# Gated-branch projection by seven products: where the partial sums of a pair of column blocks are kept

## The chip, the core and the metric

The kernel runs on one core of one Trainium2 chip. The metric is the device time of one execution in microseconds (us); several runs are taken and the median stands for the kernel. Five engines take part: TensorE (PE, matmuls into PSUM, with its weight loads PEld), VectorE (DVE), ScalarE (ACT), GpSimd (POOL) and SyncE (SP, which only issues DMAs). Each engine works through its own queue in order, and semaphores tie the queues together. SBUF holds the tiles; PSUM is eight banks of 128 x 512 fp32, which PE writes and DVE and ACT read and write.

## What is computed

One block of an encoder, in fp32, for 1024 positions of width 1024 (`norm` is an RMS norm, `mod` six vectors from a small conditioning input):

```python
h = rms_norm(x, norm_mix_g) * (1.0 + sc1) + sh1
b_s, c_s, v_s, v_c, gl_c, gate_br = split(h @ w_in)            # 7 x 1024 columns
y_a = (b_s * causal_dwconv(c_s * v_s, conv_short_w)) @ w_short_out   # 3 taps
u   = causal_dwconv(v_c * sigmoid(gl_c), conv_conf_w) + conv_conf_b  # 31 taps
y_b = silu(layer_norm(u)) @ w_conf_out
g_a, g_b = split(sigmoid(gate_br))
x = x + g1 * ((g_a * y_a + g_b * y_b) @ w_o)
h2 = rms_norm(x, norm_ffn_g) * (1.0 + sc2) + sh2
a, b = split(h2 @ w_ffn_in)
x = x + g2 * ((silu(a) * b) @ w_ffn_out);  return rms_norm(x, final_norm_g)
```

## The kernel before

**Layout.** Activations lie transposed: channels on the 128 partitions, positions along the row, in two halves of 512 (`halves`). A weight unit is a tile of 128 x 1024. To keep fp32 accuracy each operand is split in a rounded high part and the rest (`wh` by ACT, line 219; `wl` by a subtraction, line 220), and every product is three matmuls: high x high (L314), high x low part of the activation (L315), low part of the weight x high (L317).

**The projection.** The first columns of `w_in` are done as plain products (tiles `lead` and `gb`). The other 48 blocks of 128 columns are done in twelve **duals**, counted from 0. A dual takes two pairs of column blocks, p = 0 and 1 (list `PAIRS`), and does each 2 x 2 block product with seven products instead of eight, in the order `PRODUCTS = "1265734"` (M1, M2, M6, M5, M7, M3, M4). A product has two halves, one for each pair, of 4 x 3 matmuls of 128 x 512. M1, M6, M7 and M4 add up in a bank called x, M5 and M3 in z, M2 stands alone in y: three banks for each of the two pairs, six in all, taken at M1, M2 and M5 from a pool of six, so that x, y and z keep their places from dual to dual. The other two PSUM banks (`c0`, `c1`) hold the sums of the long convolution.

**The four results of a pair** are M1+M2, M1+M6+M5+M3 and two more with M7 and M4. `win_evac` (lines 647 to 712) reads the banks after each half of a product. ACT copies x to SBUF after M1 and after M6 (L673) and z after M5 (L688); DVE adds y, x and z to those copies after M2, M7 and M3 (`plus`, L633). Then comes what the kind of pair wants: `p` (c_s and v_s) multiplies the two blocks (L637) and runs the three-tap convolution; `q` (two blocks of b_s) multiplies onto that convolution's result (L683, L637) and stores it; `u` (v_c and gl_c) makes a sigmoid on ACT and multiplies (L679, L703); `g` (gates) makes sigmoids (L685, L695, L701) and stores them. In lines 637, 679 and 703 the factor `z` or `sig` is a copy in SBUF, not the bank. `short_conv` (L622 to 628) scales a row of 1024 on ACT into an SBUF tile (L624) and adds two taps to it on DVE, 1024 wide (L626).

**Weights of a dual.** `dual_units` loads four blocks by SP and lets POOL make the sums of blocks (L239, L241, L243 and, for M3, L260) and all seven `wl`. A weight unit is asked for two products ahead (`AHEAD`); there are three `wh` and three `wl` buffers and five `raw` ones, so a unit's cast waits until the product three before it is done, and the loads of a dual wait until POOL has read the last unit of the one before. POOL's order is L239, L241, `wl` of M1, L243, `wl` of M2, L260, then `wl` of M6, M5, M7, M3, M4.

**The long convolution** (31 taps, eight channel blocks) runs on DVE meanwhile: two differences (L742, L743), one start (L756) and 46 taps (L751) a block, each tap a multiply-add of 128 x 512 with its sum in `c0` or `c1`. Their places in DVE's queue are given by `reads`, the list of the `plus` instructions: tap n of block j is put behind read `(j * 47 + n) * 70 / (8 * 47)` of 72. When a block is done, `add_conv` (L765 to 772) puts its store in ACT's queue (L769) and its two adds into `tot` in POOL's (L772), behind weight unit `(j + 1) * 70 * 7 / 48 + 5`, counted through the duals, seven to each.

**Late work.** Sigmoids that nobody waits for, and the stores of gates, are collected in `late` and issued with the next ACT copy of M1, M6 or M5 (`gates`, L641 to 645). A scheduler then merges the instructions of each engine into its queue under these orders.

Of the kernel before, what the change touches and what calls it, by code (L numbers as in the profile page):

```python
# [35 lines left out]
ALU = mybir.AluOpType  # L38

P = 128  # L40
# [53 lines left out]

CONV_READS = 70

# [24 lines left out]
def block_kernel(ctx: ExitStack, tc: tile.TileContext, x0, xT, c, vecs, ada, w_first, w_plain, w_duals,  # L121
# [499 lines left out]

    def short_conv(j, p):  # L622
        sc[j] = uc_tile(f"sc{j}", T)
        nc.scalar.activation(sc[j], p[:, :T], AF.Copy, scale=col(V_SW, j))  # L624
        for s in range(1, SK):
            nc.vector.scalar_tensor_tensor(  # L626
                out=sc[j], in0=p[:, s : s + T], scalar=col(V_SW + s * KC, j), in1=sc[j], op0=ALU.mult, op1=ALU.add
            )

    reads = []  # L630

    def plus(out, ps, b):
        reads.append(nc.vector.tensor_tensor(out, ps, b, ALU.add).ins)  # L633

    def minus_times(out, a, b):

        nc.vector.scalar_tensor_tensor(out=out, in0=a, scalar=-1.0, in1=b, op0=ALU.mult, op1=ALU.mult)  # L637

    late = []

    def gates(ins):  # L641

        with tc.issue_after(ins):
            while late:
                late.pop(0)()

    def win_evac(pairs):

        st = [{} for _ in pairs]

        def start(e, kind, j):
            if kind == "u":
                u.append(u_tile(j))
                e["b"] = [u[j][:, CK - 1 + h * H : CK - 1 + (h + 1) * H] for h in range(2)]
            elif kind == "p":
                e["p"] = uc_tile(f"p{j}", T + SK - 1)
                nc.vector.memset(e["p"][:, : SK - 1], 0.0)
                e["b"] = [e["p"][:, SK - 1 + h * H : SK - 1 + (h + 1) * H] for h in range(2)]
            elif kind == "g":
                e["t"] = [uc_tile("sig", T) for _ in range(2)]  # L660
                e["b"], e["c"] = ([t[:, s] for s in halves] for t in e["t"])

        def evac(i, m, ps):
            kind, j, *rest = pairs[i]
            e = st[i]
            if m == "1":
                start(e, kind, j)
                if kind == "q":
                    e["b"] = [g_tile("m")]
            if m == "6" and kind == "q":  # L670
                e["b"].append(g_tile("v"))
            if m in "16":
                gates(nc.scalar.copy(e["b"][m == "6"], ps).ins)  # L673
            elif m in "23":
                h = m == "3"
                b = e["b"][h]
                plus(b, ps, b)
                if kind == "u" and h:
                    nc.vector.tensor_tensor(b, b, e["z"], ALU.mult)  # L679
                elif kind == "p" and h:  # L680
                    minus_times(b, e["z"], b)
                elif kind == "q":
                    nc.vector.tensor_tensor(sc[j][:, halves[h]], b, sc[j][:, halves[h]], ALU.mult)  # L683
                elif kind == "g":
                    late.append(lambda: nc.scalar.activation(b, b, AF.Sigmoid))  # L685
            elif m == "5":
                e["z"] = e["c"][1] if kind == "g" else g_tile("z")
                gates(nc.scalar.copy(e["z"], ps).ins)  # L688
            elif m == "7":
                z = e["z"]  # L690
                plus(z, ps, z)
                if kind == "u":
                    nc.scalar.activation(z, z, AF.Sigmoid, scale=-1.0)
                elif kind == "g":
                    late.append(lambda: nc.scalar.activation(z, z, AF.Sigmoid, scale=-1.0))  # L695
                elif kind == "q":
                    minus_times(sc[j + 1][:, halves[1]], e["z"], sc[j + 1][:, halves[1]])
            else:
                if kind in "ug":
                    sig = e["c"][0] if kind == "g" else g_tile("sig")  # L700
                    nc.scalar.activation(sig, ps, AF.Sigmoid, scale=-1.0)  # L701
                if kind == "u":
                    nc.vector.tensor_tensor(e["b"][0], e["b"][0], sig, ALU.mult)  # L703
                elif kind == "p":
                    minus_times(e["b"][0], ps, e["b"][0])
                    short_conv(j, e["p"])
                elif kind == "q":
                    minus_times(sc[j + 1][:, halves[0]], ps, sc[j + 1][:, halves[0]])
                    for i in range(2):
                        q_store(j + i)  # L710
                else:
                    late.append(lambda: [nc.scalar.dma_start(gate_dram[g], t) for g, t in zip((j, *rest), e["t"])])
        return evac
# [7 lines left out]
    def q_split(j, h):  # L721

        hi, q = qT[j][h]
        nc.scalar.copy(hi, f32(q))
        with tc.issue_after(reads[-1]):
            nc.vector.tensor_tensor(q, f32(q), f32(hi), ALU.subtract)
# [7 lines left out]
    TAPS = CK // 2 * 3 + 2  # L734

    def conv(j):
# [4 lines left out]
        with tc.issue_after(reads[j * CONV_READS // KC]):  # L741
            nc.vector.tensor_tensor(d, ev, od, ALU.subtract)  # L742
# [4 lines left out]
        def tap(out, src, s, wt, acc):  # L747
            nonlocal n
            n += 1
            with tc.issue_after(reads[(j * TAPS + n) * CONV_READS // (KC * TAPS)]):  # L750
                tap.ins = nc.vector.scalar_tensor_tensor(  # L751
                    out=out, in0=src[:, s : s + H], scalar=wt, in1=acc, op0=ALU.mult, op1=ALU.add
                ).ins

        with tc.issue_after(reads[j * CONV_READS // KC]):
            nc.vector.tensor_scalar(a0, od[:, :H], wsum[:, j : j + 1], col(V_CB, j), ALU.mult, ALU.add)  # L756
# [8 lines left out]
    def add_conv(j):  # L765

        hi, lo = pool_los[min((j + 1) * CONV_READS * 7 // (6 * KC) + 5, 7 * n_duals + 1)]
        with tc.issue_after(hi):
# [565 lines left out]
```

## Time and profile before

| what | value |
|---|---|
| median of 3 runs | 1500.69 us (1497.21 to 1502.33) |
| the profiled execution | 1500.65 us, its span 1498.9 us |
| granted TensorE clock, mean | 0.994 |
| stage of the twelve duals | 110.51 to 582.76 us of the span |
| in that stage busy: DVE, ACT, POOL | 437.12, 164.67, 355.12 us |

The span runs from the first to the last instruction; the execution's time has 1.75 us around it. A row of a group reads: line, engine, operation, output<-inputs, shapes, count | busy us, mean ns of one | idle time of the engine before them and what ended it. A row of a timeline reads: start, us, engine, line, operation, and in brackets the idle time before it and what ended that. A row of waits reads: who <- whom: us in total, times, longest.

### The profile page before, as it was taken

How to read it: one execution, taken by the hardware profiler on the slowest of the kernel's cores; microseconds unless marked ns; L12 is line 12 of the kernel's file. 1: busy time of each engine (PE TensorE's matmuls, PEld its weight loads, DVE VectorE, ACT ScalarE, POOL GpSimd, SP SyncE). 2: the span in 40 equal slices, each digit the busy share in tenths (PEclk: the TensorE clock that was granted, in tenths of full speed). 3: DMA queues.
4: the chain of work that ended last, by engine and by line, in shares of the span. 5: the costliest groups of instructions: out<-in, count | busy, mean ns of one | idle time of the engine just before them, and what ended most of it. 6: DMA issues, size and time to landing. Idle time of an engine off the chain costs nothing.

```text
span 1498.9 us, 17818 instructions
## 1 busy us (share of the span) xinstructions
PE 1476.3 (98%) x6523; PEld 1212.1 (81%) x6523; DVE 1190.0 (79%) x1573; ACT 591.0 (39%) x845; POOL 557.6 (37%) x467
## 2 busy tenths in 40 slices
PE   8999999999999999999999999999999999999997
PEld 5888878878878878888888887888888888888887
DVE  7997898999999997759775699877777665677755
ACT  4753333333333235226334474444444443222235
POOL 0046777778788684310121101100010016544105
PEclk9999999999999999999999999999999999999999
DMA  9412213223212159447663525555554449998403
GB/s 355 169 62 71 99 57 126 71 85 98 90 52 93 48 180 362 156 159 239 199 217 115 160 96 196 186 181 171 182 180 163 150 150 356 364 315 258 144 24 113
DMA packets 82698, 243.26 MB, mean 162 GB/s; under 512 B 9521, under 2 KB 11697, under 8 KB 82610
## 3 DMA queue, kind: packets, MB, share of 16 engines
q1 hardware_dynamic: 41776, 133.91, 26.9%
q0 software_dynamic: 36944, 95.44, 19.3%
q10 hardware_dynamic: 3890, 12.78, 2.1%
q8 instruction: 51, 0.84, 0.2%
q14 instruction: 37, 0.30, 0.1%
HBM read 179.70 MB, written 62.39 MB: 162 GB/s over the span
## 4 chain that ended last, share of the span: by engine, by line
PE 87%; DVE 5%; POOL 4%; issue 1%; DMA 1%; ACT 1%; POOLq 0%; ACTq 0%; DVEq 0%
PE x L317 11%; PE x L314 11%; PE x L315 11%; PE z L314 6%; PE z L315 6%; PE z L317 6%; PE y L317 4%; PE y L314 4%; PE y L315 4%; PE ya L314 2%; PE yb L317 2%; PE yb L314 2%; PE ya L315 2%; PE ya L317 2%; PE yb L315 2%; POOL wl L220 2%
## 5 line engine op out<-in xcount | busy, mean ns | idle before, releaser
L219 ACT CAST wh<-raw 128x1024 fp32r<-128x1024 f32 (+2 forms) x248 | 250.2, 1009 | 482.8 <-PE z L315 111.7
L220 POOL TENSOR_TENSOR wl<-raw,wh 128x1024 fp32r<-128x1024 f32 x92 | 237.3, 2587 | 95.4 <-ACT wh L219 91.3
L220 DVE TENSOR_TENSOR wl<-raw,wh 128x1024 fp32r<-128x1024 f32 (+2 forms) x156 | 177.6, 1139 | 36.5 <-ACT wh L219 35.1
L751 DVE SCALAR_TENSOR_TENSOR c<-diff,vec,c 128x512 f32<-128x512 f32 x232 | 172.2, 750 | 4.0
L1050 POOL DMA_DIRECT2D hid<-stage x71 | 37.9, 534 | 347.4 <-DVE stage L354 340.8
L314 PE MATMUL x<-th,wh 128*128 128x512 f32 x336 | 130.9, 390 | 0.0
L317 PE MATMUL x<-th,wl 128*128 128x512 f32 x336 | 130.7, 389 | 0.0
L315 PE MATMUL x<-tl,wh 128*128 128x512 f32 x336 | 130.7, 389 | 0.0
L751 DVE SCALAR_TENSOR_TENSOR c<-u,wsum,c 128x512 f32<-128x512 f32 x112 | 84.0, 750 | 4.5 <-issue 2.5
L239 POOL TENSOR_TENSOR raw<-raw 128x1024 f32<-128x1024 f32 x12 | 29.5, 2455 | 128.6 <-DVE wl L220 91.4
L317 PE MATMUL x<-t2h,wl 128*128 128x512 f32 x184 | 72.4, 395 | 3.6 <-POOL wl L220 3.6
L314 PEld LDWEIGHTS x<-th,wh 128*128 128x128 f32 x336 | 63.1, 188 | 13.6 <-DVE z L633 0.3
L317 PEld LDWEIGHTS x<-th,wl 128*128 128x128 f32 x336 | 63.1, 188 | 13.1
L315 PEld LDWEIGHTS x<-tl,wh 128*128 128x128 f32 x336 | 63.1, 188 | 13.0
L314 PE MATMUL x<-t2h,wh 128*128 128x512 f32 x184 | 72.3, 394 | 1.2 <-ACT wh L219 1.2
L315 PE MATMUL x<-t2l,wh 128*128 128x512 f32 x184 | 72.1, 393 | 0.0
L353 ACT CAST stage<-g 128x512 fp32r<-128x512 f32 x62 | 38.3, 621 | 71.2 <-DMA hid<-stage 37.6
L314 PE MATMUL z<-th,wh 128*128 128x512 f32 x168 | 65.4, 389 | 0.0
L315 PE MATMUL z<-tl,wh 128*128 128x512 f32 x168 | 65.4, 389 | 0.0
L317 PE MATMUL z<-th,wl 128*128 128x512 f32 x168 | 65.4, 389 | 0.0
L354 DVE TENSOR_TENSOR stage<-g,stage 128x512 fp32r<-128x512 f32 x62 | 42.3, 687 | 27.1 <-ACT stage L353 27.0
L1076 POOL DMA_DIRECT2D th<-hid x71 | 38.1, 537 | 49.8 <-PE x L317 29.8
(840 smaller groups left out, 4089.6 us busy)
## 6 DMA issues: line engine op xcount, KB each, us to landing
hid<-stage POOLq DMA_DIRECT2D x71, 512.0 KB, 4.7
raw<-in_w_fi SPq DMA_DIRECT2D x51, 512.0 KB, 3.8
raw<-in_w_duals SPq DMA_DIRECT2D x48, 512.0 KB, 3.5
th<-hid POOLq DMA_DIRECT2D x71, 256.0 KB, 5.7
tl<-hid POOLq DMA_DIRECT2D x71, 256.0 KB, 5.8
ada<-in_ada SPq DMA_DIRECT2D x24, 512.0 KB, 6.2
raw<-in_ada SPq DMA_DIRECT2D x24, 512.0 KB, 4.4
raw<-in_w_fo SPq DMA_DIRECT2D x24, 384.0 KB, 5.7
```

Source lines behind the costliest of these rows:

```text
L219: hi = nc.scalar.copy(wh, raw)
L220: lo = lo_engine.tensor_tensor(wl, raw, f32(wh), ALU.subtract)
L239: eng.tensor_tensor(a["s1"], a["21"], a["22"], ALU.add)
L314: nc.tensor.matmul(ps, wh, xh, start=first, stop=False, skip_group_check=again)
L315: nc.tensor.matmul(ps, wh, xl, start=False, stop=False, skip_group_check=again)
L317: mm3.ins = nc.tensor.matmul(ps, wl, xh, start=False, stop=last, skip_group_check=again).ins
L353: t_split.act = nc.scalar.copy(hi, src).ins
L354: t_split.ins = nc.vector.tensor_tensor(lo, src, f32(hi), ALU.subtract).ins
L751: tap.ins = nc.vector.scalar_tensor_tensor(out=out, in0=src[:, s : s + H], scalar=wt, in1=acc, op0=ALU.mult, op1=ALU.add).ins
L1050: nc.gpsimd.dma_start(hid_dram[key], s)
L1076: nc.gpsimd.dma_start(t, hid_dram[key][:, s])
```

## The change

- **M2 onto M1.** After each half of M1, ACT copies bank x into bank y of the same pair (PSUM to PSUM), and M2's matmuls add onto it (`onto="2"`: they don't clear the bank). The DVE add after M2 goes. For `p` and `u` ACT then copies y to SBUF; `q` multiplies straight from the bank; `g` takes its sigmoid straight from the bank.
- **Sums in PSUM.** After M3 the add is written back into bank z (except for `g`), after M7 of `q` into bank y, and the multiply that follows reads that bank. `u` writes the sigmoid of M4 over bank x. So each multiply has one operand in PSUM.
- **The short convolution** writes ACT's scaled rows into the two x banks (512 each), adds the first tap there and writes the second to SBUF: two ACT and four DVE instructions of 512 instead of one and two of 1024. It is issued late, behind the copy of M1's second half in the next dual.
- **The banks.** Six tiles are made once (`ring`); dual d takes `ring[(d + i) % 3]` for x, y, z, so the next dual's x is this one's y, its y this one's z, its z this one's x.
- **Places of the taps.** `reads` now holds every DVE instruction that reads a bank, with a time in duals; a tap goes behind the last one whose time is not over `(j * 47 + n) * 11.5 / (8 * 47)`. The first taps may start at once. `add_conv` counts `int((j + 1) * 11.5 * 7 / 8) + 5`: units 15, 25, 35, 45, 55, 65, 75, 85 instead of 15, 25, 35, 45, 56, 66, 76, 85.
- **Late work** is issued after the copy of the second half only.

In the built program PE's and POOL's instructions are the same in kind and number. POOL's order differs in three places: the adds of block 4 stand behind M4's `wl` of dual 7 (before: around L243 of dual 8), those of block 5 behind M6's `wl` of dual 9 (before: behind M5's), those of block 6 between M3's and M4's `wl` of dual 10 (before: behind M4's).

```diff
-    def product(banks, m, t, evac=None, between=None, y_tile=ps2_tile, z_tile=ps_tile):
+    def product(banks, m, t, evac=None, between=None, y_tile=ps2_tile, z_tile=ps_tile, onto=""):
...
-            if m in "125":
+            if (b, p) not in banks:
                 banks[b, p] = {"x": ps_tile, "y": y_tile, "z": z_tile}[b](b)
...
-                mm3([ps], slice(c0, c0 + P), w, [t[k]], m in "125" and k == 0, k == n - 1, m in "6734")
+                mm3([ps], slice(c0, c0 + P), w, [t[k]], m in "125" and m not in onto and k == 0, k == n - 1, m in "6734" + onto)
...
-    def short_conv(j, p):
+    def short_conv(j, p, banks):
         sc[j] = uc_tile(f"sc{j}", T)
-        nc.scalar.activation(sc[j], p[:, :T], AF.Copy, scale=col(V_SW, j))
-        for s in range(1, SK):
...
+        for h, ps in enumerate(banks):
+            nc.scalar.activation(ps, p[:, h * H : (h + 1) * H], AF.Copy, scale=col(V_SW, j))
+        for h, ps in enumerate(banks):
+            for s in range(1, SK):
+                nc.vector.scalar_tensor_tensor(
+                    out=ps if s < SK - 1 else sc[j][:, halves[h]], in0=p[:, h * H + s : (h + 1) * H + s],
+                    scalar=col(V_SW + s * KC, j), in1=ps, op0=ALU.mult, op1=ALU.add,
+                )
+    reads = [(0.0, t_split.ins)]
...
+        def evac(i, m, ps):
+            plus.ins = None
+            read(i, m, ps)
+            if plus.ins:
+                reads.append((d + (2 * PRODUCTS.index(m) + i + 1) / (2 * len(PRODUCTS)), plus.ins))
...
+            if m in "165":
+                if m == "5":
+                    e["z"] = e["c"][1] if kind == "g" else g_tile("z")
+                copy = nc.scalar.copy({"1": banks["y", i], "6": e.get("b", [0, 0])[1], "5": e.get("z")}[m], ps)
+                if i:
+                    run_late(copy.ins)
+            elif m == "2":
                 start(e, kind, j)
                 if kind == "q":
+                    times(sc[j][:, halves[0]], ps, sc[j][:, halves[0]])
+                elif kind == "g":
+                    nc.scalar.activation(e["b"][0], ps, AF.Sigmoid)
+                else:
+                    nc.scalar.copy(e["b"][0], ps)
+            elif m == "7":
+                z = banks["y", i] if kind == "q" else e["z"]
+                plus(z, ps, e["z"])
...
+            elif m == "3":
+                b, z = e["b"][1], e["z"]
                 if kind == "u":
                     nc.scalar.activation(z, z, AF.Sigmoid, scale=-1.0)
+                plus(b if kind == "g" else ps, ps, b)
+                if kind == "u":
+                    times(b, ps, z)
+                elif kind == "p":
+                    minus_times(b, ps, z)
...
+            elif kind == "u":
+                nc.scalar.activation(ps, ps, AF.Sigmoid, scale=-1.0)
+                times(e["b"][0], ps, e["b"][0])
+            elif kind == "p":
+                minus_times(e["b"][0], ps, e["b"][0])
+                late.append(lambda: short_conv(j, e["p"], [banks["x", p] for p in range(2)]))
...
+    ring = [[ps_tile("bank") for _ in range(2)] for _ in "xyz"]
     for d in range(n_duals):
-        banks, evac = {}, win_evac(PAIRS[2 * d : 2 * d + 2])
+        banks = {(b, p): ring[(d + i) % 3][p] for i, b in enumerate("xyz") for p in range(2)}
+        evac = win_evac(d, PAIRS[2 * d : 2 * d + 2], banks)
         for i, m in enumerate(PRODUCTS):
-            product(banks, m, th[m], evac, y_tile=ps_tile)
+            product(banks, m, th[m], evac, onto="2")
```

More of the change, by code (lines that the diff above doesn't have):

```diff
@@ L645, in gates, with win_evac @@
                 late.pop(0)()
-    def win_evac(pairs):
+    def win_evac(d, pairs, banks):
         st = [{} for _ in pairs]
@@ new lines, in read @@
+                if kind == "u":
+                    times(b, ps, z)
+                elif kind == "p":
+                    minus_times(b, ps, z)
+                elif kind == "q":
+                    times(sc[j][:, halves[1]], ps, sc[j][:, halves[1]])
+                else:
+                    late.append(lambda: nc.scalar.activation(b, b, AF.Sigmoid))
+            elif kind == "u":
[4 more added lines that the diff above has]
+                late.append(lambda: short_conv(j, e["p"], [banks["x", p] for p in range(2)]))
+            elif kind == "q":
+                minus_times(sc[j + 1][:, halves[0]], ps, sc[j + 1][:, halves[0]])
+                for n in range(2):
+                    q_store(j + n)
+            else:
+                nc.scalar.activation(e["c"][0], ps, AF.Sigmoid, scale=-1.0)
+                late.append(lambda: [nc.scalar.dma_start(gate_dram[g], t) for g, t in zip((j, *rest), e["t"])])
@@ L724, in q_split @@
         nc.scalar.copy(hi, f32(q))
-        with tc.issue_after(reads[-1]):
+        with tc.issue_after(reads[-1][1]):
             nc.vector.tensor_tensor(q, f32(q), f32(hi), ALU.subtract)
@@ L734, in block_kernel, with read_at @@
     TAPS = CK // 2 * 3 + 2
+    def read_at(t):
+        return max((r for r in reads if r[0] <= t), key=lambda r: r[0])[1]
     def conv(j):
```

68 lines of the change are left out of this document (16 added, 52 removed).

## The prediction

> **What bounds the kernel now.** I read the page's busy line first, then what TensorE waited for, then the projection stage dual by dual.
>
> ```profile
> PE 1476.3 (98%) x6523; PEld 1212.1 (81%) x6523; DVE 1190.0 (79%) x1573; ACT 591.0 (39%) x845; POOL 557.6 (37%) x467
> ```
>
> TensorE (PE) is busy for 98% of the span, and the change leaves its 6523 matmuls as they are. So the only time to be had is idle or slow time of PE. The view of PE's waits inside the stage of the duals (us in total, times, longest) has two rows:
>
> ```profile
> PE x L317 <- POOL wl L220: 6.2, 3, 2.6
> PE y L317 <- POOL wl L220: 2.5, 2, 2.2
> ```
>
> All five waits are for `wl`, the low part of a weight unit that GpSimd (POOL) makes. The windows below run from the first matmul of a dual to the first of the next (columns: length, busy time of PE, PEld, DVE, ACT, POOL with counts, granted clock, DMA; a count takes in a straddling matmul or two). The first row is the whole stage, the second an undisturbed dual, then duals 2, 5, 8 and 11, and last two pieces with a low clock.
>
> ```profile
> 110.51:582.76 472.25, 463.52 (x2017) 381.34 (x2016) 437.12 (x549) 164.67 (x221) 355.12 (x147) 0.99 0.30 101
> 148.59:186.67 38.08, 38.08 (x170) 31.53 (x168) 33.88 (x42) 13.31 (x18) 28.60 (x12) 1.00 0.28 97
> 186.67:229.32 42.65, 40.02 (x169) 32.62 (x168) 41.94 (x54) 12.40 (x16) 32.54 (x14) 0.96 0.19 62
> 305.48:345.39 39.91, 38.67 (x170) 31.38 (x168) 36.85 (x49) 13.79 (x18) 31.30 (x14) 1.00 0.28 93
> 421.55:463.75 42.20, 39.99 (x170) 32.58 (x168) 38.12 (x47) 12.11 (x15) 31.85 (x14) 0.96 0.19 63
> 540.12:582.76 42.64, 40.00 (x169) 32.59 (x168) 41.16 (x58) 24.41 (x39) 27.68 (x12) 0.96 0.79 285
> 202.18:205.59 3.41, 3.41 (x10) 2.67 (x9) 3.34 (x6) 0.59 (x1) 3.25 (x2) 0.50 0.40 147
> 543.51:546.92 3.41, 3.41 (x9) 2.63 (x10) 3.30 (x6) 1.09 (x2) 3.41 (x2) 0.50 0.27 111
> ```
>
> An undisturbed dual takes 38.08 us (a product 5.44, one of its halves 2.72, a matmul 0.227). Twelve take 457.0, and the stage takes 472.25, so **15.3 us** are lost: 4.57 in dual 2, 1.83 in dual 5, 4.12 in dual 8, 4.56 in dual 11, and 0.2 in the other eight. Of the 15.3, 8.7 are the waits. About 5.1 are the clock: behind the stalls of duals 2, 8 and 11 (each over 2 us) stands a piece of 3.41 us at 0.50, which costs 1.7 each time; behind the shorter waits of dual 5 stands none. The last 1.5 is what five restarts of the matmul pipe cost. These 15.3 us are the most that the change can bring.
>
> **Why POOL is late.** Ahead of each dual POOL has a burst: three weight sums (L239, L241, L243), a fourth for M3 (L260), and the `wl` of M1, M2 and M6. In dual 2 two adds of a finished convolution (L772) stand inside it. POOL's timeline (start, us), and DVE's beside it:
>
> ```profile
> 177.44 2.41 POOL L239 TENSOR_TENSOR raw<-raw 128x1024 f32<-128x1024 f32 x1 [3.54 <-DMA raw<-in_w_duals]
> ...
> 191.09 1.30 POOL L772 TENSOR_TENSOR tot<-tot,u 128x512 f32<-128x512 f32 x1
> 192.35 3.38 POOL L260 TENSOR_TENSOR raw<-raw 128x1024 f32<-128x1024 f32 x1
> 195.69 1.75 POOL L772 TENSOR_TENSOR tot<-tot,u 128x512 f32<-128x512 f32 x1
> 197.40 3.34 POOL L220 TENSOR_TENSOR wl<-raw,wh 128x1024 fp32r<-128x1024 f32 x1
> ```
> ```profile
> 180.33 2.90 DVE L637 SCALAR_TENSOR_TENSOR p<-z,p 128x512 f32<-128x512 f32 x1
> ...
> 193.40 2.89 DVE L703 TENSOR_TENSOR u<-u,sig 128x512 f32<-128x512 f32 x1
> ```
>
> In lines 637 and 703 `z` and `sig` are SBUF copies. A DVE instruction of this size takes 0.68 to 0.75 us when one operand is a PSUM bank (lines 633, 751 below); with both in SBUF, beside a POOL instruction, it takes up to 2.9, and the POOL instruction behind it 3.4 where others take 2.40. The groups of the stage (mean ns of one):
>
> ```profile
> L626 DVE SCALAR_TENSOR_TENSOR sc<-p,vec,sc 128x1024 f32<-128x1024 f32 x16 | 38.1, 2380 | 0.0
> L637 DVE SCALAR_TENSOR_TENSOR p<-z,p 128x512 f32<-128x512 f32 x8 | 19.3, 2415 | 0.0
> L703 DVE TENSOR_TENSOR u<-u,sig 128x512 f32<-128x512 f32 x5 | 12.2, 2434 | 0.0
> L633 DVE TENSOR_TENSOR z<-x,z 128x512 f32<-128x512 f32 x17 | 11.7, 687 | 20.9 <-PE x L317 20.8
> L751 DVE SCALAR_TENSOR_TENSOR c<-diff,vec,c 128x512 f32<-128x512 f32 x229 | 170.0, 750 | 3.9
> ```
>
> **The change, part by part.** *Operands in PSUM.* The 29 instructions of L626, L637 and L703 become 16 half-size pairs (32 at 0.75 us) and 13 at 0.69, all with a bank operand: 69.6 us become 33. The adds of M2 go (24 at 0.68, 16.4 us). DVE falls by 53 us, from 437 of 472 to about 384 of 457. What touches SBUF alone in the stage is then the two differences that open a convolution, the splits and small memsets.
>
> *Dual 2.* Without those partners (and with convolution 1's opening differences planned for 1.44 duals, ahead of it) the burst is seven instructions at 2.4, two adds at 1.28 and 0.4 of gaps: 19.8 us from 177.44, so M6's `wl` stands at 197.2 and not at 200.74. M6's third matmul wants it at 197.55 + 0.45 = 198.0. The stall goes: -4.57. What is late next there is nothing nearer than 0.8 us.
>
> *Dual 5* keeps its adds around L243:
>
> ```profile
> 296.60 2.65 POOL L239 TENSOR_TENSOR raw<-raw 128x1024 f32<-128x1024 f32 x1 [3.90 <-DMA raw<-in_w_duals]
> ...
> 304.51 1.28 POOL L772 TENSOR_TENSOR tot<-tot,u 128x512 f32<-128x512 f32 x1
> ```
>
> Five at 2.4, two at 1.28 and 0.3 of gaps put M2's `wl` at 311.5; it is wanted at 305.48 + 5.89 = 311.4. I leave a stall of 0.4 with its restart (between 0 and 1.8): -1.4.
>
> *Dual 8.* The new count puts the adds of convolution 4 behind dual 7's last `wl`, so ahead of the burst instead of inside it:
>
> ```profile
> 406.37 2.40 POOL L220 TENSOR_TENSOR wl<-raw,wh 128x1024 fp32r<-128x1024 f32 x1 [3.02 <-ACT wh L219]
> 412.45 2.41 POOL L239 TENSOR_TENSOR raw<-raw 128x1024 f32<-128x1024 f32 x1 [3.68 <-DMA raw<-in_w_duals]
> ...
> 420.12 1.74 POOL L772 TENSOR_TENSOR tot<-tot,u 128x512 f32<-128x512 f32 x1
> ```
>
> There POOL idles 3.68 us for a transfer, which hides 2 x 1.28. The burst loses both adds, at least 1.74 and 1.28, against a wait of 2.2 (the longest of the second row of waits): -4.12.
>
> *Dual 11.* ACT, POOL:
>
> ```profile
> 523.35 0.63 ACT L685 ACTIVATE sig<-sig 128x512 f32<-128x512 f32 x1 [7.14 <-DVE sig L633]
> ```
> ```profile
> 525.00 2.42 POOL L220 TENSOR_TENSOR wl<-raw,wh 128x1024 fp32r<-128x1024 f32 x1 [7.16 <-ACT wh L219]
> 527.36 1.27 POOL L856 DMA_DIRECT2D ga<-gate_a  x2
> ...
> 535.68 2.41 POOL L239 TENSOR_TENSOR raw<-raw 128x1024 f32<-128x1024 f32 x1 [0.66 <-DMA raw<-in_w_duals]
> ```
>
> A sigmoid in ACT's queue waited 7.14 us for DVE's add of M2, the cast of M3's weights stood behind it, POOL behind that, and the next burst began 4.4 us ahead of its dual (540.12) instead of 9.2 (177.44 against 186.67). After the change that sigmoid reads M2's bank itself, so nothing in ACT's queue waits for DVE there. Two adds (2.6) and two DMA issues (1.3 together) now stand between the `wl` of M3 and M4 in dual 10. M3's ends 19.8 us into the dual, so M4's begins at 23.7 instead of 22.8, and the burst comes 8.3 us ahead: -4.56.
>
> *What is added.* M2 starts on ACT's copy of M1, so PE waits for ACT, and behind a waiting matmul stands the whole kernel. ACT's order in each dual of the changed program is copy of M1's first half, cast of M5's weights, copy of the second half. The nearest rows, in dual 4 (M1 ends at 272.84):
>
> ```profile
> 272.87 1.05 ACT L219 CAST wh<-raw 128x1024 fp32r<-128x1024 f32 x1 [1.96 <-PE x L315]
> 273.82 0.58 ACT L673 COPY sig<-x 128x512 f32<-128x512 f32 x1
> ```
>
> The second copy ends at 274.40, and M2's second half begins at 272.84 + 2.72 = 275.56: 1.16 us to spare. The first copy has 2.72 - 0.58 = 2.1, less what the cast of M6 ahead of it takes when POOL's L243 is late. A copy into PSUM has no row; its bounds are 0.58 (the same copy into SBUF) and 1.15 (twice the width), and both fit. I take 0.58 and a cost of 0; if the cover went, each us would cost 12 (rivals). Thirteen more copies (M2 of the p and u pairs, 0.58 each) lie in ACT's idle time: it is busy 164.67 of 472.25.
>
> The short convolution now holds the two x banks that M5 of the next dual takes, 16.3 us after that dual's start. It begins behind the copies of M1 (7.0) and its own two (1.2), takes 4 x 0.75 on DVE, and with an M2 multiply ahead of it ends at about 12: 4 us to spare. The other bank changes give room: M1 no longer takes the bank that M4 has just left. The store of convolution 5 stands ahead of a copy of M1 in dual 9; the plan ends that convolution 0.4 of a dual (14 us) earlier.
>
> **Sum.** 15.3 less 0.4 in dual 5 and 0.2 that may stay: -14.7. The profiled execution took 1500.65 us (span 1498.9 and 1.75 around it), within 0.1 of the median of the three runs (1500.69): 1500.65 - 14.7 = **1486.0 us**.
>
> **Rivals.**
> *Half of it.* POOL's lengthening has another cause than DVE, and the bursts of duals 2 and 5 stay late. Only the moved adds and ACT's freed queue pay: 4.12 + 4.56, 1492.0. For it: in dual 2 the change leaves the adds where they are. Against it: the long POOL instructions stand beside the long DVE ones.
> *The clock stays.* The three slow pieces come by themselves and not from the stalls: 1486.0 + 5.1 = 1491.1. Against it: all three follow a stall of over 2 us, and none stands elsewhere in the stage. [...]
> *A new wait on ACT (slower).* The copies into PSUM are slow, or held up behind a cast. A copy of 1.74 us uses up the 1.16; from 3.0 us on the twelve second halves lose the 15.3 again. At 4 us the sum is 12 x (4 - 1.74) = 27.1: 1485.4 + 27.1 = 1512.5. Against it: every copy that has a row takes under 0.6.
> *It does not do it.* DVE's order stays late, the short convolution or the stores hold PE as much as POOL did: within 4.5 us of 1500.65. For it: DVE is still the fullest engine behind PE, at 84%.
>
> **How the numbers follow.** Forecast 0.72; half of it 0.12; the clock 0.04; does not do it 0.07; new wait 0.05. The first three are faster by over 0.3% (4.5 us, about what a measurement of this kernel can tell from no change): 0.88. The fourth is no change, 0.07; the fifth slower, 0.05. The range starts 3 us under the forecast (the full 15.3, and the runs of before lie up to 3.5 under their median) and ends over the two middle rivals with 1.5 us for the runs: 1483.0 to 1493.5.
>
> **What would show it.** No wait of PE for `wl` over 0.5 us in the stage, the granted clock at 1.00 through it, duals at 38.1 us, and the stage at about 458. POOL's L260 and L220 at 2.4; no DVE group of the stage over 1 us but the differences and splits; DVE's busy time in it under 390. Two adds of `tot` in the gap ahead of dual 8's burst. A wait of PE for an ACT copy, or for DVE at M5, would show the forecast wrong, as would a stall of dual 2 that stays with DVE's long rows gone.

## The result and the profile after

The changed kernel ("after") takes **1486.84 us** (median of four runs, 1485.55 to 1489.12) against 1500.70 (four, 1497.21 to 1502.33): a ratio of 0.9912, 95% interval 0.9891 to 0.9934. The forecast was 1486.0, in a range of 1483.0 to 1493.5. The profiled execution is the fastest of the four: 1485.55 us, its span 1483.8.

The page's busy line, then the windows of the stage and of duals 2, 5, 8 and 11 (columns as in the prediction):

```profile
PE 1469.9 (99%) x6523; PEld 1209.2 (81%) x6523; DVE 1148.4 (77%) x1565; ACT 598.6 (40%) x866; POOL 533.6 (36%) x467
```
```profile
110.89:567.85 456.96, 456.96 (x2018) 378.50 (x2016) 397.17 (x545) 172.66 (x242) 330.00 (x147) 1.00 0.30 104
187.05:225.13 38.08, 38.08 (x170) 31.54 (x168) 32.21 (x47) 12.77 (x17) 28.64 (x14) 1.00 0.21 70
301.29:339.37 38.08, 38.08 (x170) 31.54 (x168) 32.13 (x44) 14.34 (x20) 28.61 (x13) 1.00 0.29 97
415.53:453.61 38.08, 38.08 (x170) 31.54 (x168) 33.41 (x50) 12.76 (x17) 26.72 (x12) 1.00 0.23 80
529.77:567.85 38.08, 38.08 (x170) 31.54 (x168) 35.35 (x40) 23.94 (x39) 22.36 (x10) 1.00 0.81 307
```

In the first row the length equals PE's busy time: twelve times 38.08, and the view of PE's waits has no row in this stage. All 15.3 us of the prediction's budget are gone (472.25 to 456.96), and the granted clock is 1.00 in every row. No idle or slow time of PE is left in this stage.

POOL's burst ahead of dual 2 (timeline: start, us), and POOL's groups of the stage; the two rows of before under them are the same groups there:

```profile
178.00 2.40 POOL L240 TENSOR_TENSOR raw<-raw 128x1024 f32<-128x1024 f32 x1 [3.73 <-DMA raw<-in_w_duals]
...
191.32 2.39 POOL L261 TENSOR_TENSOR raw<-raw 128x1024 f32<-128x1024 f32 x1
193.68 1.28 POOL L794 TENSOR_TENSOR tot<-tot,u 128x512 f32<-128x512 f32 x1
194.92 4.76 POOL L221 TENSOR_TENSOR wl<-raw,wh 128x1024 fp32r<-128x1024 f32 x2
```
```profile
L221 POOL TENSOR_TENSOR wl<-raw,wh 128x1024 fp32r<-128x1024 f32 x84 | 204.6, 2442 | 85.7 <-ACT wh L220 78.5 <-PE bank L318 5.5 <-DMA raw<-in_w_short 1.6
L261 POOL TENSOR_TENSOR raw<-raw 128x1024 f32<-128x1024 f32 x12 | 29.1, 2427 | 0.9
L794 POOL TENSOR_TENSOR tot<-tot,u 128x512 f32<-128x512 f32 x14 | 17.9, 1289 | 0.0
```
```profile
L260 POOL TENSOR_TENSOR raw<-raw 128x1024 f32<-128x1024 f32 x12 | 34.6, 2885 | 0.9
L772 POOL TENSOR_TENSOR tot<-tot,u 128x512 f32<-128x512 f32 x14 | 23.2, 1671 | 0.4 <-DVE u L751 0.4
```

No POOL instruction of the burst is long now: the fourth sum takes 2.39 where it took 3.38, and the two `wl` of the last row 4.76 together where one took 3.34. The first of them, M6's, ends 1.06 us before M6's third matmul starts (0.8 forecast).

DVE's groups that took the place of L626 (L631), L637 (L647) and L703 (L643), an add (L640), and two that still have both operands in SBUF (L764, L744):

```profile
L764 DVE TENSOR_TENSOR diff<-u 128x527 f32<-128x527 f32 x8 | 13.2, 1647 | 0.1
...
L631 DVE SCALAR_TENSOR_TENSOR bank<-p,vec,bank 128x512 f32<-128x512 f32 x16 | 11.3, 752 | 2.3 <-ACT bank L628 2.3
...
L640 DVE TENSOR_TENSOR z<-bank,z 128x512 f32<-128x512 f32 x13 | 9.0, 689 | 24.1 <-PE bank L318 24.1
...
L647 DVE SCALAR_TENSOR_TENSOR p<-bank,z 128x512 f32<-128x512 f32 x8 | 5.5, 691 | 0.2
...
L643 DVE TENSOR_TENSOR u<-bank,u 128x512 f32<-128x512 f32 x5 | 3.5, 691 | 7.0 <-ACT bank L719 7.0
...
L744 DVE TENSOR_TENSOR q71l<-q71l,q71h 128x512 fp32r<-128x512 f32 x1 | 2.9, 2901 | 0.0
```

Where there is a bank operand, 0.69 to 0.75 us, as forecast. The copy of M1 into the bank, its group and the second half in dual 1:

```profile
L687 ACT COPY bank<-bank 128x512 f32<-128x512 f32 x24 | 13.8, 577 | 6.4 <-PE bank L318 6.0 <-ACT sig L493 0.4
```
```profile
154.44 1.05 ACT L220 CAST wh<-raw 128x1024 fp32r<-128x1024 f32 x1 [1.98 <-PE bank L316]
155.39 0.58 ACT L687 COPY bank<-bank 128x512 f32<-128x512 f32 x1
```

It takes 0.577 us on average (0.58 forecast), and the one in dual 1 ends at 155.97, 1.16 us ahead of M2's second half (157.13).

POOL ahead of dual 8 (start 415.53) and of dual 11 (start 529.77):

```profile
402.70 2.54 POOL L794 TENSOR_TENSOR tot<-tot,u 128x512 f32<-128x512 f32 x2
...
521.44 2.40 POOL L240 TENSOR_TENSOR raw<-raw 128x1024 f32<-128x1024 f32 x1 [3.72 <-DMA raw<-in_w_duals]
```

The two adds now stand ahead of dual 8's burst, and the burst of dual 11 begins 8.3 us ahead of its dual, both as forecast.

### The profile page after: what moved, and what is told of

It is laid out like the page before. It is cut to its first block, busy times and chain, and to the rows that moved or that the text cites. A ratio compares the mean times of both kernels' runs of the same rounds, so it can differ in the third digit from the quotient of the medians.

```text
span 1483.8 us, 17806 instructions
## 1 busy us (share of the span) xinstructions
PE 1469.9 (99%) x6523; PEld 1209.2 (81%) x6523; DVE 1148.4 (77%) x1565; ACT 598.6 (40%) x866; POOL 533.6 (36%) x467
## 4 chain that ended last, share of the span: by engine, by line
PE 94%; DVE 3%; ACT 1%; issue 1%; DMA 0%; POOL 0%; ACTq 0%; POOLq 0%; DVEq 0%
PE bank L316 10%; PE bank L318 10%; PE bank L315 10%; PE x L318 7%; PE x L316 7%; PE x L315 7%; PE z L318 4%; PE z L316 4%; PE z L315 4%; PE y L316 3%; PE y L315 3%; PE y L318 3%; PE ya L316 2%; PE ya L315 2%; PE yb L318 2%; PE yb L315 2%
## 5 line engine op out<-in xcount | busy, mean ns | idle before, releaser
L315 PE MATMUL bank<-th,wh 128*128 128x512 f32 x288 | 112.0, 389 | 0.0
L316 PE MATMUL bank<-tl,wh 128*128 128x512 f32 x288 | 112.0, 389 | 0.0
L318 PE MATMUL bank<-th,wl 128*128 128x512 f32 x288 | 112.0, 389 | 0.0
L315 PEld LDWEIGHTS bank<-th,wh 128*128 128x128 f32 x288 | 54.1, 188 | 11.3
L316 PEld LDWEIGHTS bank<-tl,wh 128*128 128x128 f32 x288 | 54.1, 188 | 11.2
L318 PEld LDWEIGHTS bank<-th,wl 128*128 128x128 f32 x288 | 54.1, 188 | 11.2
L315 PE MATMUL x<-th,wh 128*128 128x512 f32 x144 | 56.0, 389 | 0.0
L316 PE MATMUL x<-tl,wh 128*128 128x512 f32 x144 | 56.0, 389 | 0.0
L318 PE MATMUL x<-th,wl 128*128 128x512 f32 x144 | 56.0, 389 | 0.0
L315 PE MATMUL yb<-zsh,wh 128*128 128x512 f32 x128 | 49.8, 389 | 0.0
```

Source lines behind the costliest of these rows:

```text
L315: nc.tensor.matmul(ps, wh, xh, start=first, stop=False, skip_group_check=again)
L316: nc.tensor.matmul(ps, wh, xl, start=False, stop=False, skip_group_check=again)
L318: mm3.ins = nc.tensor.matmul(ps, wl, xh, start=False, stop=last, skip_group_check=again).ins
```

## Experiments

The stage begins at 110.5 to 114.5 us in the twelve profiled executions, with no pattern that the profiles explain, so the runs are compared by what each loses in the stage: the length of a dual, from its first matmul to that of the next, less 38.08 us. The losses are those of one profiled execution of each kernel, the medians those of 4 to 10 executions; the ratios are to executions of the kernel before that were taken with them. Part of a loss behind a long wait hangs on chance, as the last section shows.

| kernel | median, us | stage lost | dual 0 | 2 | 5 | 8 | 10 | 11 |
|---|---|---|---|---|---|---|---|---|
| before | 1500.7 | 15.29 | 0 | 4.57 | 1.83 | 4.12 | 0.21 | 4.56 |
| after | 1486.84 | 0 | 0 | 0 | 0 | 0 | 0 | 0 |
| before, places of the adds (e2) | 1500.85 | 13.30 | 0 | 4.68 | 2.14 | 0 | 2.22 | 4.26 |
| before, M2 onto M1 (e6) | 1499.26 | 14.14 | 2.12 | 3.03 | 1.32 | 6.51 | 0.89 | 0.27 |
| before, M3's sum in its bank (e12) | 1494.87 | 7.66 | 0 | 2.29 | 0.74 | 4.62 | 0 | 0.01 |
| before, late short convolution (e11) | 1491.85 | 2.74 | 0 | 1.14 | 0.04 | 0.92 | 0 | 0.64 |
| before, the last two (e13) | 1487.71 | 0.44 | 0 | 0.44 | 0 | 0 | 0 | 0 |
| after, old places of the adds (e1) | 1486.92 | 0.01 | 0 | 0 | 0 | 0.01 | 0 | 0 |
| after, SBUF operands (e3) | 1487.84 | 0.29 | 0 | 0.26 | 0.02 | 0 | 0 | 0 |
| after, SBUF operands at the old place (e8) | 1491.24 | 3.38 | 0 | 2.19 | 1.19 | 0 | 0 | 0 |
| after, taps spread by index (e7) | 1489.02 | 2.13 | 2.11 | 0 | 0.02 | 0 | 0 | 0 |
| after, longer copies (e5) | 1493.5 | 6.05 | 0.20 | 1.79 | 1.58 | 0.30 | 0.33 | 0.26 |

The theory was the prediction's: DVE instructions with both operands in SBUF lengthen POOL's (2.40 us to 3.38 ahead of M6 in dual 2 of before), and the operands in PSUM end it (duals 2 and 5); the moved adds win dual 8; ACT's freed queue wins dual 11. The rival: each is won by something else that the change does.

**The places of the adds.** In after they go back:

```diff
-        hi, lo = pool_los[min(int((j + 1) * CONV_DUALS * 7 / KC) + 5, 7 * n_duals + 1)]
+        hi, lo = pool_los[(15, 25, 35, 45, 56, 66, 76, 85)[j]]
```

> The kernel after, with one thing undone: the adds of a finished convolution go behind the weight units of before (15, 25, 35, 45, 56, 66, 76, 85), so convolution 4's two adds stand inside dual 8's burst again. If dual 8 was won by moving them, as the prediction credits it, its wait for the low part of a weight comes back: up to +4.1, about 1490. If it was won by POOL and DVE no longer lengthening one another, dual 8 becomes like dual 5 of the kernel after, which keeps its adds inside the burst and shows 0.69 us of slack: no stall, or one below 0.4, 1486 to 1487.

Measured: 1486.92 us, ratio 0.99 (0.9886 to 0.9915); dual 8 has the adds in its burst and loses 0.01. The other way round, the kernel before with the units (15, 25, 35, 45, 55, 65, 75, 85):

> The kernel before, with one thing of the change alone: the adds of the finished convolutions go behind units 15, 25, 35, 45, 55, 65, 75, 85. If the place of the adds wins dual 8 by itself, 4.1 go and about 1496.5 are left, with duals 2 and 5 as before (4.6 and 1.8). If the lengthening of POOL's instructions decides in dual 8 too, its burst stays late by part of it: 1497 to 1500. Dual 11 may move by up to 1, since convolution 6's adds come ahead of another unit.

Measured: 1500.85, ratio 0.9993 (0.9983 to 1.0002). Its windows of duals 8 and 10:

```profile
423.65:461.73 38.08, 38.08 (x170) 31.53 (x169) 37.69 (x47) 11.99 (x15) 29.68 (x12) 1.00 0.20 69
499.81:540.11 40.30, 38.67 (x169) 31.38 (x168) 39.98 (x45) 12.22 (x16) 29.51 (x14) 1.00 0.23 79
```

Dual 8 is won, as forecast, and dual 10 lost: there convolution 6's adds stand ahead of M4's `wl`, behind a `wl` of M3 that is still late (it waited 7.15 us for ACT), and wait 2.87 us more for DVE. So the edit does in dual 8 what the prediction credited it with, but it is not needed in after, and alone it is not shown to be worth anything: the stage loses 2.0 us less, and the ratio's interval takes in 1.

**Operands back in SBUF.** In after, the multiplies behind M3 and behind `u`'s M4, and the short convolution in one piece of 1024 (still late, behind the copy of M1):

```diff
-                plus(b if kind == "g" else ps, ps, b)
+                plus(b, ps, b)
...
-                    times(b, ps, z)
+                    times(b, b, z)
...
-                    minus_times(b, ps, z)
+                    minus_times(b, z, b)
...
-                times(e["b"][0], ps, e["b"][0])
+                sig = g_tile("sig")
...
+                times(e["b"][0], e["b"][0], sig)
```

> The kernel after, with the multiplies behind M3 and behind u's M4 and the short convolution back on two SBUF operands; M2 onto M1, the bank places, the spread of the taps and the places of the adds stay. By the prediction's mechanism (DVE instructions with both operands in SBUF lengthen the POOL instruction beside them) POOL's sums and low parts go from 2.4 back to as much as 3.4 us and the stalls of duals 2 and 5 come back: +3 to +6.4, 1490 to 1493. If what was won there came from DVE's lower load or its order alone, the bursts stay in time: 1486 to 1488, since DVE still lacks the 24 adds of M2.

Measured: 1487.84, ratio 0.9912 (0.9895 to 0.9928), 0.3 us lost, and not the 3 to 6.4 of the prediction's mechanism. **With the rest of the change in place, duals 2 and 5 do not need the operands in PSUM.** The long instructions are back, and so are long POOL instructions (36 over 2.6 us in the stage; before 39, after 8), but the longest stand elsewhere. DVE in dual 2, which starts at 188.50:

```profile
198.10 2.89 DVE L629 SCALAR_TENSOR_TENSOR sc<-p,vec,sc 128x1024 f32<-128x1024 f32 x1
```

The short convolution begins 9.6 us into the dual, when M6's `wl`, the last of the burst, has already begun (197.50; it takes 2.41), and the two `wl` behind it take 3.40 each, which stalls nobody; in before it began 4.8 us in, ahead of M3's sum. That pointed to its place. The theory was mended: only what lies inside the burst, from the first sum to M6's `wl` (18 us in this run, not the 14 of the next expectation), stalls PE. The next run puts the same short convolution back where it stood:

```diff
-                late.append(lambda: short_conv(j, e["p"], [banks["x", p] for p in range(2)]))
+                short_conv(j, e["p"], None)
```

> The kernel of the run with two SBUF operands, and with the short convolution put back where it stood before: straight behind the last multiply of p, not behind ACT's copy of the next M1. Theory now: DVE's long instructions lengthen POOL's wherever they stand, but only those inside the 14 us from the first weight sum to M6's low part stall PE; the late short convolution was enough to get out of that stretch. Then stalls come back, in dual 2 above all (slack there 0.06 us): +2 to +7 over that run, 1489 to 1494. Rival: what was won in duals 2 and 5 is the 24 adds of M2 taken off DVE; then it stays at 1487 to 1488.

Measured: 1491.24, ratio 0.9944 (0.9926 to 0.9962); duals 2 and 5 lose 2.19 and 1.19. POOL and DVE in dual 2 (start 188.09):

```profile
189.39 3.38 POOL L221 TENSOR_TENSOR wl<-raw,wh 128x1024 fp32r<-128x1024 f32 x1
192.72 2.28 POOL L791 TENSOR_TENSOR tot<-tot,u 128x512 f32<-128x512 f32 x1
194.96 2.85 POOL L261 TENSOR_TENSOR raw<-raw 128x1024 f32<-128x1024 f32 x1
```
```profile
188.10 2.42 DVE L629 SCALAR_TENSOR_TENSOR sc<-p,vec,sc 128x1024 f32<-128x1024 f32 x1
...
191.09 2.75 DVE L629 SCALAR_TENSOR_TENSOR sc<-p,vec,sc 128x1024 f32<-128x1024 f32 x1
...
193.77 1.78 DVE L639 TENSOR_TENSOR u<-u,sig 128x512 f32<-128x512 f32 x1
```

A `wl` of 2.40 becomes 3.38, an add of 1.29 becomes 2.28, a sum 2.85, each beside one of the three DVE rows. In after, where the instructions in their place have a bank operand and take 0.69 to 0.75 us, the same burst has an add of 1.28, a sum of 2.39 and two `wl` of 4.76 together. That the one engine lengthens the other's instructions is read from what stands beside what. DVE still lacks the 24 adds of M2 in this run, so its lower load is not what won these duals.

**One part alone, in the kernel before.** The place: the short convolution unchanged, but issued behind ACT's copy of M1's second half.

```diff
+                if m == "1" and i:
+                    with tc.issue_after(copy):
+                        while convs:
+                            convs.pop(0)()
...
-                    short_conv(j, e["p"])
+                    convs.append(lambda: short_conv(j, e["p"]))
```

> The kernel before, with one thing changed: the short convolution (two SBUF operands, full width) begins behind ACT's copy of the second half of the next M1. By the theory it leaves POOL's burst: dual 8's low part of M2 is no longer lengthened (4.1 falls to below 1), dual 2 loses 1 to 2 of its 4.6, dual 5 up to 1 of its 1.8, dual 11 keeps its 4.6 (it has no p pair): 1494 to 1497. If the place of the short convolution does not matter, 1500.

Measured: 1491.85, ratio 0.9939 (0.9925 to 0.9954), better than expected: dual 11, which was to keep its 4.6, loses 0.64. All of PE's waits in the stage:

```profile
PE x L317 <- POOL wl L220: 1.2, 2, 0.8
PE y L317 <- POOL wl L220: 0.6, 1, 0.6
```

Dual 11 shows why the sigmoid of the prediction waited 7.14 us. It waits for DVE, which comes late to the adds of M2 in dual 10. In the kernel before (dual 10 starts at 501.83) the first of them stands behind the short convolution, `u`'s multiply and six taps (4.70 us):

```profile
510.01 2.77 DVE L626 SCALAR_TENSOR_TENSOR sc<-p,vec,sc 128x1024 f32<-128x1024 f32 x1
512.70 2.89 DVE L703 TENSOR_TENSOR u<-u,sig 128x512 f32<-128x512 f32 x1
...
520.12 0.68 DVE L633 TENSOR_TENSOR m<-y,m 128x512 f32<-128x512 f32 x1
```

ACT and DVE in the run with the late short convolution, dual 10 (start 497.40):

```profile
516.17 0.64 ACT L690 ACTIVATE sig<-sig 128x512 f32<-128x512 f32 x1 [4.38 <-DVE sig L633]
```
```profile
513.06 0.69 DVE L633 TENSOR_TENSOR m<-y,m 128x512 f32<-128x512 f32 x1
```

The first add of M2 comes 15.7 us into the dual, against 18.3 before (520.12 less 501.83), the wait falls from 7.14 to 4.38, and the next burst starts 6.8 us ahead of its dual instead of 4.4.

The operand: in the kernel before, M3's sum stays in bank z and the multiply reads it there. The short convolution and `u`'s M4 keep their two SBUF operands and their place.

```diff
-                plus(b, ps, b)
+                s = ps if h and kind != "g" else b
+                plus(s, ps, b)
...
-                    minus_times(b, e["z"], b)
+                    minus_times(b, s, e["z"])
```

> The kernel before, with one thing changed: the sum of M3 stays in its bank and the multiply behind it (of p, u and q) reads it there, so L637's z form and the multiplies by z of u and q have a PSUM operand; the short convolution and M4's multiply of u keep two SBUF operands and their place. By the theory the low part of M1 ahead of duals 2, 5 and 8 goes from 2.86 to 2.40 and in dual 2 one sum from 2.75 to 2.40: the waits there shrink by 0.5 to 0.8, and where that brings them from 2.2 or 2.6 us to under 2 the 1.7 us of half clock behind them go too: dual 2 4.6 to 2 or 3.8, dual 5 1.8 to 1.3, dual 8 4.1 to 2, dual 11 as it is or 1 less; 1494 to 1497. If the length of POOL's instructions has another cause, 1500.

Measured: 1494.87, ratio 0.9954 (0.9937 to 0.997). M1's `wl` ahead of dual 8 takes 2.42 where it took 2.86, and duals 2 and 5 shrink as expected or more. Dual 11, which was to lose 1 us less at most, is clear: in dual 10 the short convolution and `u`'s multiply are as long as before (2.77 and 2.89), but DVE comes to the convolution 1.7 us into the dual and not 6.3, and to the add of M2 at 15.4. Dual 8, which was to fall to 2, stands at 4.62: its burst starts 8.1 us ahead of it (9.1 before), behind a transfer, and the short convolution now lies beside a sum too (3.40 us for 2.40). Both edits together:

> The last two single changes to the kernel before together: the short convolution behind ACT's copy of the second half of the next M1, and M3's sum left in its bank. M2 still starts afresh and is added on DVE, the banks and the spread of the taps are those of before. That run with the late short convolution lost 2.74 us in the stage (duals 2, 8 and 11); by the theory the shorter POOL instructions take the first two below 0.5: 1489 to 1491. If the operands no longer matter once the short convolution is out of the burst, 1491.5 to 1492.

Measured: 1487.71, ratio 0.9907 (0.9891 to 0.9924), better than expected. Its stage and its only wait in it:

```profile
114.33:571.73 457.40, 457.25 (x2017) 378.27 (x2016) 422.77 (x546) 165.04 (x221) 341.21 (x147) 1.00 0.29 104
```
```profile
PE x L317 <- POOL wl L220: 0.2, 1, 0.2
```

These two small edits bring 14.85 of the 15.29 us, with M2 still added on DVE and banks and taps as before. The ratio of after, 0.9912, lies inside this one's interval: neither kernel is shown to be faster than the other.

**M2 onto M1 alone**, in the kernel before (bank y taken when M1 is read; behind M2 `q`'s multiply and the gates' sigmoid read the bank, as in after):

```diff
-            if m in "16":
-                gates(nc.scalar.copy(e["b"][m == "6"], ps).ins)
-            elif m in "23":
+            if m == "1":
+                banks["y", i] = ps_tile("y")
+                gates(nc.scalar.copy(banks["y", i], ps).ins)
...
+                elif kind == "g":
+                    reads.append(nc.scalar.activation(e["b"][0], ps, AF.Sigmoid).ins)
...
+            product(banks, m, th[m], evac, y_tile=ps_tile, onto="2")
```

> The kernel before, with M2 onto ScalarE's copy of M1 alone: multiplies and short convolution on SBUF operands, banks, spread of the taps and places of the adds as before. By the prediction dual 11 is won by this part alone (no sigmoid in ACT's queue waits for DVE's add of M2): 4.6 go, about 1496, and duals 2, 5 and 8 keep their 4.6, 1.8 and 4.1. If DVE's load (16 us less) is what makes POOL late, those shrink as well: 1488 to 1494. If dual 11 was late by the adds and DMA issues of POOL itself, it stays: 1500.

Measured: 1499.26, ratio 0.9986 (0.9974 to 0.9998). Dual 11 falls to 0.27, as the prediction had it, but the time is not the 1496 expected: the new wait exists. PE's waits in the stage, and ACT ahead of M2's first half in dual 8 (start 423.26):

```profile
PE y L314 <- ACT y L674: 4.2, 4, 1.8
PE x L317 <- POOL wl L220: 2.3, 2, 1.4
PE y L317 <- POOL wl L220: 2.2, 1, 2.2
```
```profile
427.80 1.05 ACT L219 CAST wh<-raw 128x1024 fp32r<-128x1024 f32 x1 [4.45 <-POOL raw L243]
...
429.24 0.59 ACT L674 COPY y<-x 128x512 f32<-128x512 f32 x1
```

The copy stands behind M6's cast, and that behind POOL's late sum: a late POOL now stops PE by a second way, 1.0 us here, and then by `wl` as well (2.2). Dual 8 loses 6.51. So the edit that gives the change its name gains 0.14% as long as the bursts are late.

**The spread of the taps.** In after, by index over a list of 72 reads, as before:

```diff
+    adds = []
...
-            with tc.issue_after(read_at((j * TAPS + n) * CONV_DUALS / (KC * TAPS))):
+            with tc.issue_after(adds[(j * TAPS + n) * CONV_READS // (KC * TAPS)]):
```

> The kernel after, with the taps of the convolutions spread over a list of the reads of the banks, as before, instead of over time. If the spread by time keeps DVE's long opening differences out of POOL's burst and so wins a part of duals 2 and 5, stalls come back there: 1488 to 1492. If the operands in PSUM and the later short convolution suffice: 1485.5 to 1487.5, no wait for the low part of a weight over 0.5 us.

Measured: 1489.02, ratio 0.9922 (0.9907 to 0.9936). Duals 2 and 5 stay won; dual 0, which neither expectation named, loses 2.11 to the same new wait, and 1.2 us come behind the stage, a wait for POOL's `tot`. PE's wait in the stage, and ACT in dual 0 (start 110.75):

```profile
PE bank L316 <- ACT bank L689: 1.8, 1, 1.8
```
```profile
113.34 0.62 ACT L356 CAST th<-x 128x512 fp32r<-128x512 f32 x1 [7.67 <-DVE tl L357]
...
117.55 0.57 ACT L689 COPY bank<-bank 128x512 f32<-128x512 f32 x1 [0.40 <-ACT sig L494]
```

Taps stand between DVE's splits of the activations, ACT's casts wait for those splits, and the copy of M1 waits behind the casts. In after no tap stands between the last six splits, and the copy starts 3.3 us into the dual instead of 6.8.

**The price of the new wait.** In after, M1's second half is copied five times:

```diff
+                if m == "1" and i:
+                    for _ in range(4):
+                        nc.scalar.copy(banks["y", i], ps)
```

> The kernel after, with ACT copying the second half of M1 five times over into the same bank ahead of M2 (four copies of no use per dual). A copy holds ACT for about 0.5 us, so the bank is ready about 2.0 us later, 0.85 beyond the 1.16 us to spare. By the prediction's price of this wait (each us beyond the margin costs 12): 12 x 0.85 = 10, between 8 and 14, about 1497; more if the casts behind the copies come late for POOL. If the margin is not what the trace of after shows (M2 follows M1 with something else between them), 1486 or far above 1500.

Measured: 1493.5, ratio 0.9951 (0.9931 to 0.9972). Dual 2, and PE's waits in the stage:

```profile
189.25:229.12 39.87, 38.41 (x169) 31.45 (x168) 32.30 (x47) 15.04 (x21) 28.87 (x14) 1.00 0.21 67
```
```profile
PE bank L318 <- POOL wl L221: 2.8, 2, 1.5
```

Not a clean test. In dual 1 the last copy ends 1.25 us after M2's second half is due, but in this run the first five matmuls of M6 (1.13 us) stand ahead of that half and fill most of the time. Ten duals lose 0.09 to 0.33 each; in duals 2 and 5, M6 then asks for its `wl` earlier, which costs 1.3 to 1.5 more. The price of 12 us for each us was neither borne out nor refuted. The margin agrees: the four copies, 2.4 us in all, take the end from 1.16 us ahead of M2's second half to 1.25 behind it.

## Why the prediction was right, and where it was not

**The budget** (15.3 us, all of it in PE's waits for `wl`, the restarts and the half clock) held to 0.1 us, and the sum of 14.7 fell short of what came in the stage by the 0.6 it had set aside. Between the medians 13.9 us came, between the profiled executions 15.1. The clock went with the waits, so the rival "the clock stays" (1491.1) is out; not every wait of over 2 us has the slow piece behind it, though (the 2.3 us ahead of `lead` in before has none; last section). "Half of it" is out: both bursts are in time. The lengthened rows of the two runs on SBUF operands, and the shorter `wl` of M1 where M3's multiply alone reads a bank (2.42 for 2.86), put DVE beside POOL as the cause.

**Dual 2** came as computed (M6's `wl` 1.06 us early, 0.8 forecast), but the step "without those partners" gave the whole 4.57 to the operands. Two things take the partners out of the burst: the operands, and the late issue of the short convolution, which the prediction looked at only for the x banks ("4 us to spare") and priced at nothing. With the late place kept, taking the operands back costs 0.26 in this dual; in the kernel before, the place alone takes 3.4 of this dual's 4.57 and 12.55 of the 15.29 us of the stage. This is the step that failed, though the total came right: a moved instruction was checked for what waits for it, and not for what it had stood beside.

**Dual 5**: 0.4 of stall forecast, none came. M2's `wl` is 0.69 us early: the burst starts 9.26 us ahead of the dual (8.88 before), and its instructions follow one another without the 0.3 of gaps.

**Dual 8**: the moved adds do win it where the bursts are long (e2); in after, without them, it would have stood by a hair (M2's `wl` 0.21 us ahead of its matmul in e1). So the 4.12 has two cures, the moved adds or the rest of the change, and each suffices.

**Dual 11**: the chain from DVE's add over ACT's sigmoid and cast to POOL is right, and M2 onto M1 cuts it (0.27 left in e6). But the chain does harm only where DVE comes late to the add in dual 10 (18.3 us into it). Two other edits bring DVE there at 15.7 and 15.4, and with the chain still in place this dual loses 0.64 and 0.01.

**The new wait** has the size that was computed (0.577 and 1.16 us) and costs nothing in after. "A cost of 0" was argued from dual 4, though. Dual 0 has a queue of its own on ACT, and only the new spread of the taps keeps that clear (2.1 us in e7); the prediction had no price for that part.

**DVE's busy time** fell by 40 us, not by 53. The instructions that changed form cost what was forecast. Those that kept two SBUF operands got longer: the two differences from 22.6 to 26.4 us (L764 from 1436 to 1647 ns), the sixteen splits of `q` from 14.1 to 21.5, with five of over 2 us (one of them in the row above) where before there was one. Four more taps fall in the stage (3 us). On the other side the prediction left out the multiplies of `u` by `z` and of `q` (L679, L683), which also had two SBUF operands and gave back 7 us. None of this cost time.

## What to carry to other kernels

When two engines slow each other, ask where in the schedule they meet before asking how to stop it: beginning the short convolution 5 us later brought 12.55 of the 15.29 us, more than the 7.6 of rewriting the operands of the multiplies behind M3. Whether new operands for the short convolution at its old place would do as much was not tried. Terms won by removing causes don't add up; once slack is there, the second cure for the same stall brings nothing (0.01 and 0.29 us lost without it in e1 and e3), so test each part alone in the old kernel and each part undone in the new one. A new dependency that is harmless with the queues on time (M2 on ACT's copy, no wait in after) is one more way to stop the main engine when they are late (1.0 us in dual 8 of e6, 1.8 in dual 0 of e7): look at the first and the last pass of the loop too, not at a middle one.

## What the runs showed of the hardware

**What a wait of PE costs hangs on where it falls.** Ahead of the first matmuls of `lead`, long before the stage, PE waits 2.3 us in before, after, e1, e2, e3, e6 and e12, and is idle for 2.32 us in the two stretches of e13 below. In e13 the second of them is a piece of 3.41 us at half clock; in before, after and e12 the clock there is 1.00. So the length of a wait does not decide.

The slow pieces of before and of after lie on a grid. In the kernel before they begin at 7.62, 202.18, 430.87, 543.51 and, at the end, 1495.83 us, which is 57, 67, 33 and 279 steps of 3.413 us apart. In after the first begins at 8.22 us and the only other, at the end, at 1479.37, 431 steps on; the offset differs from that of before. Cut the whole execution into stretches by that grid, and take PE's idle time in the stretch that ends where a slow piece begins or could begin. The wait of e12, then its stretch and the next; the stretch of e13 and the next; and the stretch ahead of the slow piece in dual 2 of before (columns as in the prediction):

```profile
PE lead L310 <- ACT x L397: 2.3, 1, 2.3
```
```profile
17.01:20.42 3.41, 1.48 (x14) 1.29 (x12) 1.88 (x4) 0.38 (x1) 0.00 (x0) 1.00 0.70 275
20.42:23.83 3.41, 3.01 (x7) 1.44 (x8) 3.37 (x7) 0.86 (x2) 0.00 (x0) 1.00 0.44 130
```
```profile
17.29:20.70 3.41, 1.34 (x13) 1.15 (x11) 1.99 (x3) 0.51 (x1) 0.00 (x0) 1.00 0.64 257
20.71:24.12 3.41, 3.16 (x4) 1.51 (x5) 3.38 (x7) 0.86 (x2) 0.00 (x0) 0.50 0.53 151
```
```profile
198.77:202.18 3.41, 1.38 (x6) 1.16 (x7) 3.27 (x5) 0.00 (x0) 3.41 (x2) 1.00 0.08 14
```

With 1.93 us idle (3.41 less 1.48) the next stretch ran at 1.00, with 2.07 and 2.03 at 0.50. In before, the stretches ahead of the slow pieces of duals 2, 8 and 11 had 2.03, 2.21 and 2.64 us idle. In before and after, from the wait ahead of `lead` up to the last 25 us, no other stretch had more than 1.73 (after, 15.05 to 18.46 us), and the clock fell behind none of them. With the waits of 1.82, 1.86 and 1.99 us in the stage (dual 0 of e6 and e7, dual 2 of e8 and of e12) the clock of the dual was 1.00, and it lost the wait and 0.3. In dual 8 of e6, with two waits of 1.0 and 2.2 us, the clock was 0.61 from 434 to 440 us and 0.92 over the 44.59 us of the dual; that is two slow pieces by an estimate (0.08 of 44.59 is 3.6 us, and a piece at half clock costs 1.7).

A slow piece made a dual lose 1.9 us more than its wait (duals 2, 8 and 11 of before, dual 8 of e12). So a cure that brings a wait from 2.7 to 2.0 us may be worth 2.3 or 0.7 (an estimate from these figures), by where the wait fell, and the 1.7 us behind each long stall of before and of the runs built from it belong in part to luck: of the 2.63 us in its dual 2, 2.03 fell into one stretch. How much of the spread between executions comes from this was not measured, nor what lies between 1.93 and 2.03 us.
